# Counting GpSimd overlap in the assumed VectorE durations of a list-scheduled delta rule

## The chip, the cores and the metric

The kernel runs on one core of a Trainium2 chip, as one launch. The metric is the device time of that launch in microseconds (us), taken as the median of several executions. Besides the time there is one profiled execution, whose trace records every instruction of the core's engines: TensorE (PE, with its weight loads as PEld), VectorE (DVE), ScalarE (ACT), GpSimd (POOL) and SyncE (SP), which issues the DMA transfers.

## The reference

One inference step of a two-layer hybrid decoder, for a prompt of 1024 tokens and eight further sequences ("samples") of one token each. Layer one mixes by a gated delta rule with 8 heads of 128x128 state; layer two is a sliding-window attention over one shared K/V. The change lies in layer one alone:

```python
def gated_delta_rule(q, k, v, g, beta, s0):
    ...
    G = jnp.cumsum(gc, axis=-1)
    decay = jnp.exp(jnp.where(causal, G[..., :, None] - G[..., None, :], -jnp.inf))
    kb = kc * bc[..., None]
    m = jnp.where(strict, jnp.einsum('bnhid,bnhjd->bnhij', kb, kc) * decay, 0.0)
    rhs = jnp.concatenate([vc * bc[..., None], kb * jnp.exp(G)[..., None]], axis=-1)
    sol = lax.linalg.triangular_solve(eye + m, rhs, left_side=True, lower=True, unit_diagonal=True)
    ...
    def step(s, xs):
        u_i, w_i, qk_i, qd_i, kd_i, gt_i = xs
        v_new = u_i - jnp.einsum('bhcd,bhde->bhce', w_i, s)
        o_i = jnp.einsum('bhcd,bhde->bhce', qd_i, s) + jnp.einsum('bhij,bhje->bhie', qk_i, v_new)
        s = s * gt_i[..., None, None] + jnp.einsum('bhcd,bhce->bhde', kd_i, v_new)
        return s, o_i

def gdn_layer(x, conv_buf, s0, norm_g, w_in, conv_w, a_log, dt_bias, o_norm, w_out):
    proj = rmsnorm(x, norm_g) @ w_in
    qkv, gate, a, beta_logit = jnp.split(proj, [...], axis=-1)
    qkv, new_buf = causal_conv_silu(qkv, conv_buf, conv_w)      # 4 taps per channel
    ...                                                        # l2norm of q and k
    o, s_fin = gated_delta_rule(q, k, v, g, beta, s0)
    o = rmsnorm(o, o_norm) * jax.nn.silu(gate)
    return x + o @ w_out, new_buf, s_fin
```

The samples run through the same layer, each with a state of its own that is read from and written back to HBM.

## The kernel before, in words

**Stages.** Up to about 82 us the kernel loads and norms x and makes the first projections. From 82 to 752 us lies the delta-rule stage: the projections of all heads, the convolution, the delta rule, and the first part of the layer's output projection. From 752 to about 808 us the rest of that output projection runs for tiles of 128 tokens (loop over `P3O`, lines L1405 to L1455: `hx` is the residual tile, `ohl2` the split output of the last heads, `ohs` that of the samples). The attention layer takes the rest.

**Tiling of the delta-rule stage.** Each head's 1024 tokens are cut in chunks, and the chunks of a head are worked in two halves of four (512 columns on an engine); half n counts from 0 to 15 over the 8 heads. For a half, the convolution makes three taps each on VectorE (`co<-ue,cvT,co`, 528 columns) and two products on GpSimd (`ue<-ue,co`, `co<-co,ue`); the norms are small operations of four columns (`rs_x`, `rs_u`, `rkb`, `f`, `fu`); `ktok` is the normed k, transposed by TensorE into `ktp`; the triangular inverse is a series of `ivt` matmuls with `t`, `q` and `xlv` on VectorE between them; the chain over the chunks is the matmuls `chA` and `chB`; and the half's output `osb` is normed and transposed into `otp`. Everything else on TensorE is the *fill*: the projections `pj<-xg,whi`/`wlo` (weights split in a high and a low part by `whi` on ScalarE and `wlo` on VectorE), and at the end the output projection `pj<-woa,ohl` tile by tile.

**The order is a list made by the kernel itself.** The parts of the stage are generators (`chains`, `inverses`, `prep_all`, `norms`, `conv_all`, `feed`, `samples`, `proj_all`, ...) that yield one operation after the other. While the kernel is built, a class `Order` walks through them as a list scheduler. It holds for each engine the time `at[e]` until which it is busy, and for each tile when it was written and read last, by assumed durations (`took`). It always takes the operation that can start earliest by these times; ties go to the lower priority number (chains 1, convolution 5, `samples` 7, fill 9), and a TensorE operation that is not fill counts as ready 250 ns later. What it emits is the order of each engine's queue, so the assumed durations decide that order and nothing else. All these instructions carry the line of the one call that emits them, L543 (L558 after the change). The assumed duration of a convolution tap is 205 + 1.05*528 = 759 ns, whatever GpSimd does meanwhile.

**The samples' states.** `sample_batch` (lines L1147 to L1273), called by `samples` after heads 3 and 7, updates the states of four heads in eight units, each of 256 KB. Per unit: load `ssm` (SP), multiply by the decay (GpSimd, `ssm<-ssm,smp`), a matmul `up` (TensorE), add (VectorE, `ssm<-ssm,up`), store (SP, `out_7`). The tile `ssm` has two buffers, so a unit's load waits for the store of the unit two before. After the second batch's last add, VectorE's queue holds `ogm` (the samples' output), then the first `ohl2` and `hx` operations of the code behind the stage; SP's queue holds behind the last store the loads of the first four `hx` tiles. These orders behind the stage are fixed by the code.

Of the kernel before, what the change touches and what calls it, by code (L numbers as in the profile page):

```python
# [50 lines left out]
OPH = 400  # L51


D0, PEM, VF, DP = 12000.0, 250.0, 1.0, 2000


@with_exitstack
def hybrid_step(
# [9 lines left out]
    V, S, G, PE, DMA = nc.vector, nc.scalar, nc.gpsimd, nc.tensor, nc.sync  # L68
# [163 lines left out]
    with tc.tile_pool(name="p2a", reuse_waits="tile", bufs=1) as p2a, \  # L232
# [63 lines left out]
        for t in range(NT + 1):  # L296
# [9 lines left out]
            for hf in range(2):  # L306
                ps = gps("xps").rearrange("p (k t) -> p k t", k=4)
                for k in range(4):
# [4 lines left out]
                                in1=hi.bitcast(F32), op=ALU.subtract)  # L313
# [14 lines left out]
        with tc.high_priority(offset=DP):  # L328
# [29 lines left out]
            for kk in (15, 13, 11, 9, 7, 5, 3):  # L358
# [17 lines left out]
                            in1=rb.rearrange("p (c h) -> p c h", h=H), op=ALU.mult)  # L376
            psg = gps("psg")
            gfl = gf.rearrange("p h c -> p (h c)")
            for i, m in enumerate((mle, mgt, ones)):
# [8 lines left out]
                            in1=ident[:NS, :NS].unsqueeze(1).broadcast_to([NS, 2 * H, NS]), op=ALU.mult)  # L388
# [10 lines left out]
    class Op:  # L399
        __slots__ = ("e", "f", "a", "k", "use", "t")  # L400

        def __init__(self, e, f, a, k):
            self.e, self.f, self.a, self.k = e, f, a, k
            outs = [x for x in (k.get("out", a[0] if a else None), k.get("accum_out")) if x is not None]
            ins = [x for x in (*a[0 if "out" in k else 1:], *(y for n, y in k.items() if n not in ("out", "accum_out")))
                   if isinstance(x, bass.AP)]
            self.use = [(extent(x), True) for x in outs] + [(extent(x), False) for x in ins]
# [29 lines left out]
    def free_n(ap):  # L437
        n = 1
        for d_ in ap.shape[1:]:
            n *= d_  # L440
        return n

    def took(op):

        out = op.k["out"] if "out" in op.k else op.a[0]
        n = free_n(out)
        name = op.f.__name__
        if op.e == "P":
            src = op.a[2]
            n = free_n(src)  # L450
            if src.dtype == F16:
                return max(29, n / 2.4 + 2.5)
            t_ = n / 2.295 + 7 if n >= 256 else 109
            return t_ * (2 if name == "matmul" and src.dtype == F32 else 1)
        if op.e == "V":
            if name == "scalar_tensor_tensor" and n >= 64:
                return VF * (205 + 1.05 * n)
            if name == "tensor_tensor" or ap_psum(op):
                return VF * (150 + 1.04 * n)
            return VF * (150 + 0.65 * n)  # L460
        if op.e == "S":
            t_ = 165 + 0.83 * n
            if isinstance(op.k.get("scale"), bass.AP):
                t_ += 100
            return t_ + (235 if "accum_out" in op.k else 0)
        if op.e == "G":
            if name == "affine_select":
                return 130 + 1.25 * n
            if name == "tensor_tensor":
                return 100 + 2.35 * n  # L470
            return 100 + 0.8 * n if name == "memset" else 200 + 5 * n
        return 60

    def ap_psum(op):
        return any(x[0][0].space == PSUM for x in op.use)

    AFTER = {"P": 250.0, "V": 70.0, "S": 70.0, "G": 90.0}

    class Order:
        def __init__(self, slots, begin):  # L480
            self.slots, self.at = slots, dict(begin)
            self.toks = set()
            self.procs = []
            self.seen, self.rings, self.base = {}, {}, {}
            self.dma = 0.0

        def mark(self, *tok):
            self.toks.add(tok)
# [35 lines left out]

        def emit(self, op, t_):
            c_ = took(op)
            self.at[op.e] = t_ + c_
            if op.e == "D":
                n = 1
                for d_ in (op.k["out"]).shape:  # L530
                    n *= d_
                self.dma = max(self.dma, t_) + n * 4 / 180.0
                end = self.dma + 2000.0
            else:
                end = t_ + c_ + AFTER[op.e]
            for (tile_, *ext), write in op.use:
                w, rd = self.region(tile_, write).setdefault(tuple(ext), [("", 0.0), {}])
                if write:
                    self.seen[tile_.name][tuple(ext)][0] = (op.e, end)
                    rd.clear()  # L540
                else:
                    rd[op.e] = max(rd.get(op.e, 0.0), end)
            op.f(*op.a, **op.k)  # L543
# [859 lines left out]
    with tc.tile_pool(name="p3", reuse_waits="tile", bufs=2) as p3:  # L1403
# [4 lines left out]
        for t in P3O:  # L1408
# [13 lines left out]
            for ci in range(2):  # L1422
                c_ = ts(ci, 512)
# [20 lines left out]
            for hf in range(2):  # L1444
                ps = gps("hps").rearrange("p (k t) -> p k t", k=4)
                k0 = 4 * hf
                for k in range(4):
# [4 lines left out]
                                op=ALU.subtract)  # L1452
# [414 lines left out]
```

## Time and profile before

| | |
|---|---|
| time, median of 3 runs | 1298.4 us (1294.66 to 1300.23) |
| time of the profiled execution | 1299.52 us |
| its span | 1297.8 us |
| mean granted TensorE clock | 0.985 of full |
| delta-rule stage, 82 to 752 us | 670 us |
| rest of the output projection, 752 to 808 us | 56 us |

The span is what the trace covers; the execution's time is 1.7 us longer. "Granted clock" is the share of full TensorE speed that the chip let the engine run at. An engine's idle time is given with the instruction that ended it, its releaser; VectorE operations with a PSUM operand read what TensorE has just written, those without have all operands in SBUF.

### The profile page before, as it was taken

How to read it: one execution, taken by the hardware profiler on the slowest of the kernel's cores; microseconds unless marked ns; L12 is line 12 of the kernel's file. 1: busy time of each engine (PE TensorE's matmuls, PEld its weight loads, DVE VectorE, ACT ScalarE, POOL GpSimd, SP SyncE). 2: the span in 40 equal slices, each digit the busy share in tenths (PEclk: the TensorE clock that was granted, in tenths of full speed). 3: DMA queues.
4: the chain of work that ended last, by engine and by line, in shares of the span. 5: the costliest groups of instructions: out<-in, count | busy, mean ns of one | idle time of the engine just before them, and what ended most of it. 6: DMA issues, size and time to landing. Idle time of an engine off the chain costs nothing.

```text
span 1297.8 us, 24347 instructions
## 1 busy us (share of the span) xinstructions
PE 1223.9 (94%) x8887; PEld 1110.2 (86%) x8887; DVE 925.4 (71%) x2656; ACT 633.7 (49%) x1812; POOL 287.4 (22%) x404
## 2 busy tenths in 40 slices
PE   3999999999999999998999978999999999999998
PEld 3989898989999988888988756888889888888898
DVE  7468988878979897787976349587685677677221
ACT  5236555645455453545443127375574566666100
POOL 1036433424324353343301122111030020000000
PEclk9999999999999999998999979999999999999899
DMA  7021111110221322110256656111020021002322
GB/s 240 1 81 35 36 29 40 37 51 18 68 66 36 98 65 86 36 36 17 67 158 209 203 200 203 39 52 31 3 74 9 3 74 35 26 2 88 123 86 73
DMA packets 131988, 92.03 MB, mean 71 GB/s; under 512 B 33881, under 2 KB 123713, under 8 KB 131809
## 3 DMA queue, kind: packets, MB, share of 16 engines
q1 hardware_dynamic: 131868, 90.48, 23.6%
q8 instruction: 70, 1.15, 0.4%
q14 instruction: 50, 0.40, 0.1%
HBM read 69.28 MB, written 23.25 MB: 71 GB/s over the span
## 4 chain that ended last, share of the span: by engine, by line
PE 66%; DVE 20%; ACT 5%; DMA 4%; issue 3%; POOL 2%; SPq 1%; DVEq 0%; ACTq 0%; POOLq 0%
PE pj L543 24%; PE pj L100 15%; PE ivt L543 4%; DVE co L543 3%; PE chB L543 3%; PE sps L100 2%; PE chA L543 2%; PE op L100 2%; DMA out_dram<-hx 1%; PE ptp L1646 1%; DVE wqkv L82 1%; PE sp L543 1%; PE tq L1593 1%; DVE f L543 1%; PE psab L100 1%
## 5 line engine op out<-in xcount | busy, mean ns | idle before, releaser
L543 PE MATMUL pj<-xg,whi 128*128 128x384 f32 (+1 forms) x1392 | 289.3, 335 | 1.0 <-ACT whi L543 1.0
L543 PEld LDWEIGHTS pj<-xg,whi 128*128 128x128 f32 x1392 | 222.0, 190 | 2.7 <-ACT whi L543 1.2
L100 PE MATMUL pj<-wqkv,ng 128*128 128x384 f32 x768 | 154.2, 344 | 0.0
L543 PE MATMUL pj<-xg,wlo 128*128 128x384 f32 (+1 forms) x696 | 153.2, 337 | 0.0
L543 DVE SCALAR_TENSOR_TENSOR co<-ue,cvT,co 128x528 f32<-128x528 f32 x144 | 134.5, 940 | 16.1 <-ACT co L543 14.5
L100 PEld LDWEIGHTS pj<-wqkv,ng 128*128 128x128 f32 x768 | 132.3, 190 | 4.6 <-issue 4.2
L543 PEld LDWEIGHTS pj<-xg,wlo 128*128 128x128 f32 x696 | 112.9, 191 | 1.4 <-issue 0.7
L93 POOL TENSOR_TENSOR raw<-raw,gains 128x512 f32<-128x512 f32 x40 | 45.7, 1152 | 254.4 <-DMA raw<-in_w_in_b_dram 178.7
L100 PE MATMUL pj<-wob,oh 128*128 128x384 f32 (+1 forms) x576 | 97.9, 324 | 0.3 <-DVE hx L1828 0.3
L100 PEld LDWEIGHTS pj<-wob,oh 128*128 128x128 f32 x576 | 90.2, 190 | 1.1 <-DVE hx L1828 0.5
L543 PE MATMUL pj<-woa,ohl 128*128 128x512 f32 x288 | 76.1, 406 | 0.0
L543 PEld LDWEIGHTS pj<-woa,ohl 128*128 128x128 f32 x288 | 51.8, 188 | 11.5 <-issue 1.5
L1828 DVE TENSOR_TENSOR hx<-hx,pj 128x384 f32<-128x384 f32 (+3 forms) x27 | 13.7, 507 | 64.8 <-PE pj L100 35.8
L543 ACT COPY ue<-pj 128x384 f32<-128x384 f32 (+1 forms) x88 | 31.7, 377 | 52.8 <-PE pj L543 45.8
L543 POOL TENSOR_TENSOR ue<-ue,co 128x528 f32<-128x528 f32 x24 | 33.9, 1412 | 72.4 <-ACT ue L543 72.4
L543 DVE TENSOR_TENSOR wlo<-raw,whi 128x512 fp32r<-128x512 f32 x58 | 43.6, 757 | 7.6 <-ACT whi L543 7.4
L543 ACT ACTIVATE ue<-co 128x528 f32<-128x528 f32 x48 | 30.8, 644 | 30.2 <-DVE co L543 27.9
L543 ACT CAST whi<-raw 128x512 fp32r<-128x512 f32 x58 | 35.8, 619 | 16.9 <-PE pj L543 16.5
L100 PE MATMUL pj<-woa,ohl 128*128 128x512 f32 x96 | 28.7, 453 | 11.2 <-DVE ohl L1421 5.7
L543 POOL TENSOR_TENSOR co<-co,ue 128x528 f32<-128x528 f32 x24 | 39.0, 1623 | 1.3
L100 PE MATMUL sps<-kTh,qst 128*128 128x256 f32 (+1 forms) x144 | 37.5, 297 | 0.9 <-DVE m L1623 0.9
L100 PE MATMUL sps<-kTl,qst 128*128 128x256 f32 (+1 forms) x144 | 35.9, 297 | 0.5 <-DVE kTl L1600 0.5
(906 smaller groups left out, 2935.2 us busy)
## 6 DMA issues: line engine op xcount, KB each, us to landing
raw<-in_w_in_a_dram SPq DMA_DIRECT2D x64, 256.0 KB
ssm<-in_state_ssm_dram SPq DMA_DIRECT2D x32, 256.0 KB
hD<-hx SPq DMA_DIRECT2D x16, 512.0 KB
raw<-in_w_in_b_dram SPq DMA_DIRECT2D x32, 256.0 KB
xt<-in_x_prompt_dram SPq DMA_DIRECT2D x8, 512.0 KB
out_dram<-ssm SPq DMA_DIRECT2D x16, 256.0 KB
raw<-in_w_out_a_dram SPq DMA_DIRECT2D x16, 256.0 KB
hx<-in_x_prompt_dram SPq DMA_DIRECT2D x8, 512.0 KB
```

The source lines that it names most:

```text
L82: V.tensor_tensor(out=lo, in0=raw, in1=hi.bitcast(F32), op=ALU.subtract)
L93: G.tensor_tensor(out=raw, in0=raw, in1=gain[:, k:k + n].unsqueeze(2).broadcast_to([P, n, c]), op=ALU.mult)
L100: PE.matmul(out, lhsT, rhs, start=start, stop=stop, skip_group_check=True)
L543: op.f(*op.a, **op.k)
L1593: PE.transpose(tq[:, ts(h, P)], qhl[:, h].rearrange("p a d -> p (a d)"), identr)
L1646: PE.transpose(pp[:, ts(h, P)], pr[h // 2][:, h % 2, ts(kt, P)], ident)
L1828: V.tensor_tensor(out=hx[:n, :cn], in0=hx[:n, :cn], in1=ps[:n, :cn], op=ALU.add)
```

## The change

Two things are added. `shares_port` picks GpSimd's two-operand and select operations, and those VectorE operations that have a second tensor input (`in1`) and no operand in PSUM. `emit` keeps the assumed intervals of the last four such GpSimd operations, and lengthens the assumed duration of such a VectorE operation by HOLD = 0.6 of its overlap with each of them, where the operation counts as at least 500 ns long for the overlap. GpSimd's own assumed durations stay.

```diff
-D0, PEM, VF, DP = 12000.0, 250.0, 1.0, 2000
+D0, PEM, VF, DP, HOLD = 12000.0, 250.0, 1.0, 2000, 0.6
...
+    def shares_port(op):
+
+        if op.e == "G":
+            return op.f.__name__ in ("tensor_tensor", "affine_select")
+        return op.e == "V" and "in1" in op.k and not ap_psum(op)
+
...
+            self.held = []
...
         def emit(self, op, t_):
             c_ = took(op)
+            if shares_port(op):
+                if op.e == "G":
+                    self.held = self.held[-3:] + [(t_, t_ + c_)]
+                else:
+                    for b_, e_ in self.held:
+                        over = min(t_ + max(c_, 500.0), e_) - max(t_, b_)
+                        if over > 0.0:
+                            c_ += HOLD * over
             self.at[op.e] = t_ + c_
```

No instruction is added, removed or altered; only their order within the delta-rule stage moves, on every engine. Three places:

TensorE, half n = 6 (first half of the fourth head), the rows that stand behind the chain's last `chB`, as far as the transpose `otp` of the half's output (the number behind a name is that of the tile's allocation). Before:

```order
L543 MATMUL aps_5041<-co_4754,kT_5007 128x128 x2
L543 MATMUL pj_4951<-xg2_99,whi_4469 128x264
L543 MATMUL sp_5052<-kq_4734,ssm_5025 128x2 x4
L543 MATMUL pj_4951<-xg2_99,whi_4469 128x264 x3
L543 MATMUL kps_5079<-ident_78,co_4489 128x128 x4
L543 MATMUL pj_4951<-xg2_99,whi_4469 128x264 x2
L543 MATMUL pj_5101<-xg0_97,whi_4676 128x384 x4
L543 MATMUL dps_5118<-gm_5074,mgtr_116 128x512
L543 MATMUL pj_5101<-xg0_97,whi_4676 128x384 x4
L543 MATMUL pj_5101<-xg0_97,wlo_4677 128x384
L543 MATMUL dps_5118<-gm_5077,mgtr_116 128x512
L543 MATMUL otp_5125<-ident_78,osb_4875 128x128 x4
```

The same place of the changed kernel, where two fill matmuls of 264 columns, behind the same `chB`, stand ahead of these rows:

```order
L558 MATMUL qps_4964<-ident_78,co_4809 128x128 x4
L558 MATMUL pj_4930<-xg2_99,whi_4511 128x264 x8
L558 MATMUL pj_4992<-xg0_97,whi_4774 128x384 x8
L558 MATMUL pj_4992<-xg0_97,wlo_4775 128x384 x8
L558 MATMUL ktp_5036<-ident_78,ktok_4913 128x128 x4
L558 MATMUL pj_4992<-xg0_97,whi_4774 128x384 x8
L558 MATMUL pj_5062<-xg1_98,whi_4774 128x384 x2
L558 MATMUL nps_5055<-kT_5041 128x128 x4
L558 MATMUL dps_5077<-gm_4980,mgtr_116 128x512
L558 MATMUL dps_5077<-gm_4983,mgtr_116 128x512
L558 MATMUL pj_5062<-xg1_98,whi_4774 128x384 x2
L558 MATMUL otp_5086<-ident_78,osb_4782 128x128 x4
```

Between `chB` and `otp` stand 15 fill matmuls before (6 of 264 columns, 9 of 384) and 38 now (10 and 28).

TensorE, the end of the stage: the last fill (`pj<-woa1,ohl`), the `up` matmuls of the second sample batch, and the first matmul of the code behind the stage. Before:

```order
L543 MATMUL pj_9541<-woa0_8253,ohl_9487 128x512 x14
L543 MATMUL up_9565<-db_9455,kl_9054 128x512
L543 MATMUL pj_9541<-woa0_8253,ohl_9487 128x512 x4
L543 MATMUL pj_9572<-woa1_8404,ohl_9487 128x512 x18
L543 MATMUL up_9598<-db_9455,kl_9054 128x512
L543 MATMUL up_9603<-db_9455,kl_9054 128x512
L100 MATMUL pj_9639<-woa2_8663,ohl2_9636 128x512 x6
```

And in the changed kernel:

```order
L558 MATMUL pj_9512<-woa0_8199,ohl_9470 128x512 x7
L558 MATMUL up_9528<-db_9419,kl_9385 128x512
L558 MATMUL pj_9512<-woa0_8199,ohl_9470 128x512 x11
L558 MATMUL pj_9544<-woa1_8336,ohl_9470 128x512 x18
L558 MATMUL up_9568<-db_9419,kl_9385 128x512
L558 MATMUL up_9573<-db_9419,kl_9385 128x512
L558 MATMUL up_9584<-db_9577,kl_9385 128x512
L558 MATMUL up_9591<-db_9577,kl_9385 128x512
L558 MATMUL up_9598<-db_9577,kl_9385 128x512
L558 MATMUL up_9603<-db_9577,kl_9385 128x512
L100 MATMUL pj_9639<-woa2_8477,ohl2_9636 128x512 x6
```

Of the batch's eight `up` matmuls two stood behind the last fill before, and six do now; six and two stand within the fill.

SP, the same place: state loads (`ssm<-in_state_ssm`), state stores (`out_7`), the store of the last `hx` tile of the stage, weights of the next layer (`raw`), and the first `hx` load of the code behind. Before:

```order
L543 DMA hD_88<-hx_9486 128x1024
L543 DMA ssm_9575<-in_state_ssm_dram 128x4x128
L543 DMA out_7_dram<-ssm_9525 128x4x128
L91 DMA raw_10195<-in_w_in_b_dram 128x4x128
L91 DMA raw_10200<-in_w_in_b_dram 128x4x128
L91 DMA raw_10205<-in_w_in_b_dram 128x4x128
L543 DMA out_7_dram<-ssm_9575 128x4x128
L91 DMA raw_10210<-in_w_in_b_dram 128x4x128
L1413 DMA hx_9634<-hD_88 128x1024
```

And in the changed kernel, behind the three `raw` loads, which stand where they did:

```order
L558 DMA out_7_dram<-ssm_9537 128x4x128
L558 DMA ssm_9579<-in_state_ssm_dram 128x4x128
L91 DMA raw_10210<-in_w_in_b_dram 128x4x128
L558 DMA ssm_9581<-in_state_ssm_dram 128x4x128
L558 DMA out_7_dram<-ssm_9579 128x4x128
L558 DMA ssm_9588<-in_state_ssm_dram 128x4x128
L558 DMA out_7_dram<-ssm_9581 128x4x128
L558 DMA ssm_9595<-in_state_ssm_dram 128x4x128
L558 DMA out_7_dram<-ssm_9588 128x4x128
L558 DMA out_7_dram<-ssm_9595 128x4x128
L1428 DMA hx_9634<-hD_88 128x1024
```

Four more loads and four more stores now stand ahead of the `hx` loads.

## Rows read from the trace of the kernel before

**Rows 1.** The page's first part: busy time, share of the span and instructions, by engine.

```profile
PE 1223.9 (94%) x8887; PEld 1110.2 (86%) x8887; DVE 925.4 (71%) x2656; ACT 633.7 (49%) x1812; POOL 287.4 (22%) x404
```

**Rows 2.** Table by stage: window, length, busy time, granted clock, DMA share, GB/s.

```profile
82.00:752.00 670.00, 645.96 (x5246) 593.51 (x5247) 538.57 (x1156) 328.30 (x973) 229.48 (x326) 0.99 0.24 70
752.00:808.00 56.00, 43.33 (x191) 30.08 (x192) 39.12 (x124) 29.54 (x51) 13.88 (x18) 0.88 0.69 214
```

**Rows 3.** TensorE's waits from 82 to 752 us: total, times, longest.

```profile
PE ivt L543 <- DVE t L543: 3.7, 4, 1.7
PE otp L543 <- DVE m L543: 3.3, 3, 2.1
PE otp L543 <- DVE osb L543: 2.2, 2, 1.4
PE ktp L543 <- DVE ktok L543: 2.2, 1, 2.2
PE ivt L543 <- DVE q L543: 2.1, 3, 0.9
PE ivt L543 <- DVE xlv L543: 1.7, 2, 1.4
...
PE otp L543 <- DVE vt L543: 1.4, 1, 1.4
```

**Rows 4.** Table by stretch, two stretches of reduced clock in the delta-rule stage.

```profile
553.00:556.40 3.40, 3.40 (x17) 3.40 (x16) 2.63 (x4) 0.87 (x2) 3.00 (x3) 0.50 0.03 5
...
590.50:597.30 6.80, 5.91 (x38) 5.60 (x38) 6.70 (x11) 1.00 (x3) 0.84 (x4) 0.50 0.29 77
```

**Rows 5.** VectorE's operations of L543: shortest/median/longest in ns, first and last start.

```profile
L543 DVE SCALAR_TENSOR_TENSOR co<-ue,cvT,co x144: 750/768/1847, 57.0 to 621.8; 128x528 f32<-128x528 f32 x144
...
L543 DVE TENSOR_TENSOR xlv<-ivt,lm x32: 676/691/693, 134.9 to 658.4; 128x512 f16<-128x512 f32 x32
...
L543 DVE TENSOR_SCALAR rs_x<-ssq x16: 155/162/1305, 101.2 to 631.5; 128x4 f32<-128x4 f32 x16
```

**Rows 6.** Timeline at 479 to 487 us, GpSimd, VectorE and TensorE: start, length, operation, [idle before].

```profile
479.47 1.33 POOL L543 TENSOR_TENSOR ue<-ue,co 128x528 f32<-128x528 f32 x1 [4.87 <-ACT ue L543]
479.52 1.30 DVE L543 TENSOR_SCALAR rs_x<-ssq 128x4 f32<-128x4 f32 x1
486.03 0.65 PE L543 MATMUL ktp<-ident,ktok 128*128 128x128 f32 x4 [2.17 <-DVE ktok L543]
```

**Rows 7.** Timeline of TensorE at half n = 6, last chain matmul and output transpose.

```profile
386.58 0.39 PE L543 MATMUL chB<-w,dt 128*128 128x128 f32 x2
392.45 0.63 PE L543 MATMUL otp<-ident,osb 128*128 128x128 f32 x4 [0.92 <-ACT jk L543]
```

**Rows 8.** The page's costliest group: busy time, mean ns of one, idle before.

```profile
L543 PE MATMUL pj<-xg,whi 128*128 128x384 f32 (+1 forms) x1392 | 289.3, 335 | 1.0 <-ACT whi L543 1.0
```

**Rows 9.** Timeline at the stage's end, of TensorE, SP, GpSimd and VectorE, in order of time.

```profile
745.68 0.50 PE L543 MATMUL up<-db,kl 24*128 24x512 f32 x1
746.11 5.40 PE L543 MATMUL pj<-woa,ohl 128*128 128x512 f32 x22
752.71 0.38 SPq L543 DMA_DIRECT2D ssm<-in_state_ssm_dram  x1
756.49 1.04 POOL L543 TENSOR_TENSOR ssm<-ssm,smp 128x512 f32<-128x512 f32 x1 [8.05 <-DMA ssm<-in_state_ssm_dram]
757.56 0.69 DVE L543 TENSOR_TENSOR ssm<-ssm,up 128x512 f32<-128x512 f32 x1 [4.73 <-POOL ssm L543]
758.80 3.78 PE L100 MATMUL pj<-woa,ohl 128*128 128x512 f32 x8 [5.73 <-DVE ohl L1421]
759.30 2.38 SPq L1413 DMA_DIRECT2D hx<-hD  x4
765.12 1.28 DVE L1434 TENSOR_TENSOR hx<-hx,pj 128x512 f32<-128x512 f32 x2
765.95 9.26 PE L100 MATMUL pj<-woa,ohl 128*128 128x512 f32 x28 [3.37 <-DVE hx L1434]
```

## The prediction, made before the changed kernel was run

> **What bounds the kernel now.** I read the page's busy times first. TensorE works 94% of the span, VectorE 71%, GpSimd 22% [rows 1], so what a new order can change on the whole is TensorE's idle time. The table by stage then tells where there is any: from 82 to 752 us, where the change acts, TensorE is busy 645.96 of 670.00 us, 24.0 us idle; from 752 to 808 us, behind it, it is busy 43.33 of 56 us [rows 2]. The table of waits names what the 24 us are: TensorE waits for the steps of the inverse on VectorE (`ivt` for `t`, `q`, `xlv`: 3.7 + 2.1 + 1.7 = 7.5 us), for what stands on VectorE ahead of an output transpose (`otp`: 3.3 + 2.2 + 1.4 = 6.9 us), once for `ktok` (2.2 us), and for little besides [rows 3]. Two stretches of the stage run at half of the granted clock (0.50, the 1.2 of 1.2 and 2.4 GHz), right after such stalls, 3.40 and 6.80 us long [rows 4]. At full clock their work would take half, so (3.4 + 6.8)/2 = 5.1 us more are lost. The stage thus has 24.0 + 5.1 = 29 us to give at most.
>
> Does the cause that the change assumes exist? The list of VectorE's operations says so: a tap takes 768 ns in the median, near the 759 that the scheduler assumes, but up to 1847; the norm's `rs_x` takes 162 ns and up to 1305; while `xlv`, which reads PSUM, stays between 676 and 693 [rows 5]. The timeline shows how: `rs_x` starts at 479.52 and ends at 480.82, just behind GpSimd's `ue`, which ran from 479.47 to 480.80. A small operation was held for the whole of GpSimd's, and the `ktok` that hangs on it came 2.17 us late for TensorE [rows 6].
>
> **The change, part by part.** No work is added, so each term is one of place.
>
> *Stalls in the stage.* Where VectorE's operations are now assumed longer, what hangs on them is ordered later, and fill takes their place. Half n = 6 is the example. Before, TensorE comes to `otp` 392.45 − 386.58 = 5.87 us after the last chain matmul and has waited 0.92 of it [rows 7]; so 4.95 us of work stood between. The changed order puts 23 more fill matmuls there. One costs 289.3/1392 = 0.208 us [rows 8], 23 cost 4.8, which covers 0.92 several times. By the same count for all 16 halves, the work ahead of `otp` grows where halves 3 to 8 wait, and I count 5 us of the 6.9 us of `otp` waits as gone. The inverse's steps stand in the new order about as far from each other as before, so their 7.5 us and `ktok`'s 2.2 shrink by a third at most: 2 us counted, since where one overlap goes another comes. Of the 5.1 us of half clock, which hang on single stalls, I count 2. Sum −9 us. Bounds: 0, if new stalls take the place of the old; −29, if all is found.
>
> *The tail.* This is the part for which the change was not made. Before, two `up` matmuls stand behind the last fill, now six. A unit's cost where nothing covers it is in the timeline: its load is issued at 752.71, GpSimd begins at 756.49, VectorE's add ends at 757.56 + 0.69 = 758.25, 5.54 us from issue to sum [rows 9]. Before, the last unit ends there, the first split of the output (`ohl`), next in VectorE's queue, follows, and TensorE resumes at 758.80 after 5.73 us of waiting; then the four `hx` loads, which stand on SP behind the last store, go out at 759.30, the add to the first starts at 765.12, and TensorE resumes at 765.95 after 3.37 more [rows 9]. In the changed order the unit that ends at 758.25 is only the fourth of eight, and loads have two buffers, each freed by the store of the unit two before:
> unit 5: its load stands right behind that unit's store, so it goes out at about 758.7 and its sum is ready at 758.7 + 5.5 = 764.2;
> unit 6: its load waits for the landing of unit 4's store, issued at about 758.3. No row shows a store's landing alone. Below it is 0, above it is a load's way to its first user, 756.49 − 752.71 = 3.8 us [rows 9]; I take the middle, 2. Sum at 760.3 + 5.5 = 765.8;
> unit 7: waits for unit 5's store, 764.3 + 2, sum at 771.8;
> unit 8: waits for unit 6's store, 765.9 + 2, sum at 773.4.
> TensorE's first resumption moves from 758.80 to 773.4 + 0.55 = 774.0. The `hx` loads go out at about 774; before, the first was used 765.12 − 759.30 = 5.8 us after issue, with weights' transfers ahead of it and GpSimd late for the `ohs` next in VectorE's queue; alone it may take a load's 3.8 us. I take 4.4, and 0.83 from the add to TensorE as before: 779.2 against 765.95, **+13.2 us**. Bounds: no time for the store and 3.8 for `hx`, 775.6, +9.7; 3.8 for the store and 5.8 for `hx`, 784, +18. TensorE's work there stood behind long waits before too, at a granted clock of 0.88 in the mean [rows 2], so the clock is counted at no difference.
>
> *Less work ahead of the tail.* Four `up` matmuls leave the fill; one cost 746.11 − 745.68 = 0.43 us there [rows 9], in the tail they hide in waits: −1.7 us.
>
> *The second batch's reading of the states* (`sp`) now comes tens of matmuls before the end instead of hundreds, with loads that have little ahead of them. What covers them is the fill of one tile; if that is gone one load's 3.8 us shows. I take +1, bounds 0 and 4.
>
> Sum: 13.2 − 1.7 + 1 − 9 = +3.5 us on the profiled execution's 1299.5, so 1303.0. That execution is 1.1 us above the median of 1298.4, so against the median: **1302 us**.
>
> **The rivals.**
>
> *A. Stalls hardly shrink, and the tail costs its price (slower).* The rows show a block of a whole GpSimd operation: 1.30 us for work of 0.16 [rows 5, 6]. The change assumes 0.6 of an overlap, takes a small operation as 500 ns, and leaves out `rs_x`, which has one input only. What was to be late stays late, by less. Then the stalls give 3 and not 9: 13.2 − 1.7 + 1 − 3 = +9.5, 1308 us. The Trainium skill, "SBUF — State Buffer", section "Who interferes with whom", states this mechanism: VectorE's second pair of ports is GpSimd's, the lock on it is exclusive, whoever issues first has it for the whole instruction and the other fully blocks, and single-input operations such as tensor_scalar can take the pair too. The trace agrees in the 1.30 us of `rs_x`; by that rule an overlap costs all of the rest of the other engine's instruction, and its time would be rival A's 1308. For it: the rows above, and that GpSimd's own waiting is in neither list. Against it: more distance helps whatever its reason, and half n = 6 has five times what it lacked.
>
> *B. The stage gives back most of its stalls (faster).* All `otp` and `ktok` waits, half of the inverse's and all of the half clock would be 6.9 + 2.2 + 3.8 + 5.1 = 18, and with the smaller waits some 22: 13.2 − 1.7 + 1 − 22 = −9.5, 1289 us. It decides from the point where the stage gives more than 12.5 + 6.5 = 19 us. For it: all stalls hang on VectorE's being late, which is what the change teaches the list. Against it: it needs two thirds of all that there is, and a new list makes stalls of its own.
>
> *C. The tail is hidden (faster or same).* If the loads go out earlier than I work out, or the later waits behind 766 us shrink since the weights are there by then, the tail costs 5 in place of 13: 5 − 1.7 + 1 − 9 = −5, 1294 us. For it: a DMA share of 0.69 from 752 to 808 us [rows 2], so transfers are a part of those waits. Against it: two buffers, and the stores ahead of them, tie every load to the sum of two units before, whatever the bandwidth.
>
> **How the numbers follow.** About 0.5%, 6.5 us, is what a measurement of this kernel can tell from no change: 1291.9 to 1304.9. Forecast (stalls give 6 to 15, tail 10 to 16): 0.46, most of it within that bound and a part above. A: 0.27. B: 0.12. C: 0.15, half of it under 1291.9. Faster then 0.12 + 0.06 = 0.18; slower 0.27 and 0.09 of the forecast, 0.36; same 0.46. The range reaches from C's lower part to A with the tail's upper bound: 1290 to 1312; the forecast alone has 1296 to 1307.
>
> **What the changed profile would show.** The tail right: TensorE's wait for `ohl` (then L1436) of 18 to 24 us in place of 5.73, SP's issues of `ssm` loads there about 2 and 6 us apart in turn, TensorE's busy share from 752 us on lower by a fifth. The stalls right: TensorE's idle time from 82 us to the last fill at 15 us in place of 24, the `otp` waits under 2 us, the ends of the fill about 8 us earlier. Wrong: idle time of 20 us or more there (A), of under 8 (B), or TensorE's second resumption less than 8 us after the first `up` plus 14.5, as before (C). What would undo the whole working is a change in TensorE's busy time itself, which I have as equal, since its instructions are.

## The result, and the profile after

The changed kernel takes 1315.97 us in the median of 4 executions (1312.5 to 1320.2), the kernel before 1297.91, also of 4: a ratio of 1.0139, 95% interval 1.0118 to 1.0160. It is slower by 18 us, outside the range that was given, on the side of rival A but beyond it. The profiled execution took 1317.07 us, its span is 1315.3. In e1 to e4 below an execution of 1.5 to 4.6 times the usual time (one each of e1, of e3 and of the kernel before) is left out of the median.

The table by stage, with a window that ends with the fill (columns as in [rows 2]):

```profile
82.00:749.50 667.50, 645.32 (x5241) 593.74 (x5241) 531.72 (x1152) 329.75 (x973) 228.09 (x321) 0.99 0.23 67
```

TensorE is idle for 667.5 − 645.3 = 22.2 us in the stage, against 24.0 [rows 2]. So the idle time of the stage hardly changed, and the loss came behind it. The clock did not change there either: as in [rows 4], one stretch of 3.4 and one of 6.8 us stand at half clock, elsewhere than before (columns as there):

```profile
519.00:522.40 3.40, 2.80 (x25) 2.64 (x26) 1.26 (x2) 1.43 (x3) 0.66 (x1) 0.50 0.92 266
532.70:539.50 6.80, 6.30 (x22) 6.04 (x23) 5.27 (x9) 2.08 (x7) 1.89 (x5) 0.50 0.00 0
```

The waits of TensorE in the stage, now (columns as in [rows 3]):

```profile
PE dps L558 <- POOL gm L558: 2.2, 2, 1.4
PE ivt L558 <- ACT xlv L558: 1.6, 1, 1.6
PE chB L558 <- DVE rr L558: 1.6, 1, 1.6
PE chA L558 <- DVE st L558: 1.5, 4, 0.8
PE otp L558 <- DVE osb L558: 1.4, 1, 1.4
...
PE chB L558 <- ACT qs L558: 1.3, 4, 0.7
PE chB L558 <- DVE rs_u L558: 1.1, 1, 1.1
...
PE ivt L558 <- DVE t L558: 1.0, 3, 0.6
...
PE otp L558 <- DVE m L558: 0.8, 1, 0.8
```

The list of [rows 3] is another list now. `ktp` for `ktok` has gone from it, `otp` waits 1.4 + 0.8 us here where it waited 6.9, and in their place the chain matmuls `chA` and `chB` wait for `rr`, `st`, `qs` and `rs_u`. Before, they hardly waited:

```profile
PE dps L543 <- POOL gm L543: 1.5, 2, 1.3
...
PE chB L543 <- ACT qs L543: 0.7, 3, 0.3
...
PE chA L543 <- DVE st L543: 0.6, 1, 0.6
```

The VectorE operations themselves are as stretched as in [rows 5]:

```profile
L558 DVE SCALAR_TENSOR_TENSOR co<-ue,cvT,co x144: 751/766/1922, 57.0 to 630.2; 128x528 f32<-128x528 f32 x144
...
L558 DVE TENSOR_SCALAR rs_x<-ssq x16: 156/168/1253, 101.6 to 632.2; 128x4 f32<-128x4 f32 x16
```

The end of the stage, TensorE's timeline (columns as in [rows 9]):

```profile
742.04 7.03 PE L558 MATMUL pj<-woa,ohl 128*128 128x512 f32 x29
749.00 0.50 PE L558 MATMUL up<-db,kl 24*128 24x512 f32 x2
756.19 0.79 PE L558 MATMUL up<-db,kl 24*128 24x512 f32 x2 [6.69 <-POOL db L558]
762.00 0.79 PE L558 MATMUL up<-db,kl 24*128 24x512 f32 x1 [5.01 <-DVE ssm L558]
763.99 0.79 PE L558 MATMUL up<-db,kl 24*128 24x512 f32 x1 [1.20 <-DVE ssm L558]
764.71 2.08 PE L100 MATMUL pj<-woa,ohl 128*128 128x512 f32 x4
773.45 3.78 PE L100 MATMUL pj<-woa,ohl 128*128 128x512 f32 x8 [6.66 <-DVE ohl L1436]
778.12 8.47 PE L100 MATMUL pj<-woa,ohl 128*128 128x512 f32 x28 [0.89 <-DVE hx L1449]
786.43 1.04 PE L1463 MATMUL hps<-ident,hn 128*128 128x128 f32 x8
```

Of the six `up` matmuls behind the fill the first two run at once; then TensorE waits four times, 6.69 + 5.01 + 1.20 us for the others and 6.66 for `ohl`, and 0.89 for `hx`, where 5.73 and 3.37 stood in [rows 9]. From the fill's end to the second resumption it is 778.12 − 749.07 = 29.0 us; before it was 765.95 − 751.5 = 14.5. SP's queue shows why:

```profile
755.89 0.38 SPq L558 DMA_DIRECT2D out_dram<-ssm  x1
756.33 0.50 SPq L558 DMA_DIRECT2D ssm<-in_state_ssm_dram  x1
...
759.03 0.37 SPq L558 DMA_DIRECT2D ssm<-in_state_ssm_dram  x1
761.97 0.38 SPq L558 DMA_DIRECT2D out_dram<-ssm  x1
764.28 0.37 SPq L558 DMA_DIRECT2D ssm<-in_state_ssm_dram  x1
764.75 0.45 SPq L558 DMA_DIRECT2D out_dram<-ssm  x1
768.05 0.37 SPq L558 DMA_DIRECT2D ssm<-in_state_ssm_dram  x1
769.53 3.77 SPq L558 DMA_DIRECT2D out_dram<-ssm  x2
773.40 1.91 SPq L1428 DMA_DIRECT2D hx<-hD  x4
```

A load follows the store that frees its buffer by 2.3 to 3.3 us (761.97 to 764.28, 764.75 to 768.05), and the `hx` loads go out last, at 773.40 against 759.30 [rows 9]. VectorE's first add to `hx` then waits for TensorE and not for the load:

```profile
777.29 1.28 DVE L1449 TENSOR_TENSOR hx<-hx,pj 128x512 f32<-128x512 f32 x2 [2.72 <-PE pj L100]
```

The profiled executions' difference, 17.5 us of span, splits like this, from TensorE's timeline of both (the attention layer is counted from its first projection of the prompt's tokens, `pj<-wqkv,ng`):

| stretch | before | after | difference |
|---|---|---|---|
| 82 us to the fill's end | 669.5 | 667.1 | −2.4 |
| fill's end to the first `hps` transpose | 23.5 | 37.4 | +13.9 |
| from there to the first projection of the attention layer | 35.7 | 35.6 | −0.1 |
| attention layer to the end | 487.1 | 493.4 | +6.3 |

### The profile page after: what moved, and what is told of

The parts are those of the page before. It is cut to its first block, busy times and chain, and to the rows that moved or that the text cites. A ratio compares the mean times of both kernels' runs of the same rounds, so it can differ in the third digit from the quotient of the medians.

```text
span 1315.3 us, 24356 instructions
## 1 busy us (share of the span) xinstructions
PE 1228.9 (93%) x8887; PEld 1114.4 (85%) x8887; DVE 922.0 (70%) x2656; ACT 635.3 (48%) x1812; POOL 289.9 (22%) x404
## 4 chain that ended last, share of the span: by engine, by line
PE 67%; DVE 16%; ACT 6%; DMA 5%; issue 3%; POOL 2%; SPq 1%; DVEq 0%; ACTq 0%; POOLq 0%
PE pj L558 26%; PE pj L100 15%; PE ivt L558 4%; PE chB L558 3%; PE sps L100 2%; DVE co L558 2%; PE chA L558 2%; PE op L100 2%; DMA out_dram<-hx 1%; PE ptp L1661 1%; DVE wqkv L82 1%; PE sp L558 1%; PE nps L558 1%; DMA hx<-hD 1%; DMA ssm<-in_state_ssm_dram 1%
## 5 line engine op out<-in xcount | busy, mean ns | idle before, releaser
L558 PE MATMUL pj<-xg,wlo 128*128 128x384 f32 (+1 forms) x696 | 149.7, 335 | 0.0
L558 DVE SCALAR_TENSOR_TENSOR co<-ue,cvT,co 128x528 f32<-128x528 f32 x144 | 134.0, 938 | 14.4 <-ACT co L558 12.8
L558 PE MATMUL pj<-woa,ohl 128*128 128x512 f32 x288 | 79.4, 410 | 0.4 <-ACT ohl L558 0.4
L1843 DVE TENSOR_TENSOR hx<-hx,pj 128x384 f32<-128x384 f32 (+3 forms) x27 | 13.7, 508 | 66.2 <-PE pj L100 41.0
L558 ACT CAST whi<-raw 128x512 fp32r<-128x512 f32 x58 | 35.8, 619 | 18.5 <-PE pj L558 18.0
L100 PE MATMUL pj<-woa,ohl 128*128 128x512 f32 x96 | 28.8, 454 | 9.5 <-DVE ohl L1436 6.7
L558 ACT COPY w<-chB 128x128 f32<-128x128 f32 x64 | 17.0, 265 | 42.8 <-PE chB L558 42.1
```

Of the source, the lines that this page charges most:

```text
L100: PE.matmul(out, lhsT, rhs, start=start, stop=stop, skip_group_check=True)
L1843: V.tensor_tensor(out=hx[:n, :cn], in0=hx[:n, :cn], in1=ps[:n, :cn], op=ALU.add)
```

## The experiments

The columns "stage idle" (TensorE's idle time from 82 us to the fill's end), "tail" (fill's end to first `hps`) and "attention" are read from the timeline of each run's profiled execution as in the table above. Times are medians; the ratio is to the kernel before, run beside it. That kernel took 1295 to 1298 us in these rounds, so compare ratios rather than times. In the row of e3 and e15 the time is e3's, the rest that of e15's one execution, which took 1310.0 us.

| run | us | ratio, 95% interval | fill's end | stage idle | `up` behind fill | tail | attention |
|---|---|---|---|---|---|---|---|
| before | 1297.9 | | 751.5 | 24.0 | 2 | 23.5 | 487.1 |
| after | 1316.0 | 1.0139 [1.0118, 1.0160] | 749.1 | 22.2 | 6 | 37.4 | 493.4 |
| e1 after again | 1312.2 | 1.0115 [1.0066, 1.0164] | 749.0 | 22.3 | 6 | 36.9 | 493.0 |
| e2 tail alone | 1311.0 | 1.0103 [1.0066, 1.0140] | 748.6 | 23.9 | 6 | 35.8 | 486.6 |
| e3, e15 after, prefetch | 1305.8 | 1.0068 [1.0047, 1.0090] | 758.3 | 26.4 | 4 | 23.1 | 490.5 |
| e4 before, prefetch | 1300.5 | 1.0020 [1.0004, 1.0036] | 751.9 | 22.4 | 4 | 23.0 | 487.8 |
| e5 VectorE 2% longer | 1318.1 | 1.0182 [1.0147, 1.0217] | 762.2 | 30.3 | 5 | 32.4 | 485.8 |
| e6 full lock | 1358.2 | 1.0492 [1.0453, 1.0530] | 800.6 | 46.5 | 6 | 37.3 | 486.8 |
| e7 HOLD 0.3 | 1302.4 | 1.0061 [1.0043, 1.0080] | 750.6 | 23.0 | 4 | 27.0 | 485.7 |
| e8 samples early | 1311.2 | 1.0115 [1.0072, 1.0158] | 771.9 | 37.4 | 0 | 9.2 | 490.5 |
| e9 after, batch 2 at 1.3 | 1309.2 | 1.0122 [1.0066, 1.0177] | 763.3 | 27.6 | 2 | 22.6 | 488.4 |
| e10 HOLD 0.3, batch 2 at 0.5 | 1293.4 | 0.9987 [0.9970, 1.0003] | 760.2 | 26.9 | 0 | 9.2 | 484.1 |
| e11 before, batch 2 at 1 | 1289.6 | 0.9952 [0.9928, 0.9976] | 756.2 | 26.1 | 0 | 9.2 | 484.9 |
| e12 before, batch 2 at 2.1 | 1292.1 | 0.9976 [0.9960, 0.9992] | 759.6 | 27.9 | 0 | 9.2 | 483.8 |
| e13 after, 4 fills late | 1312.2 | 1.0111 [1.0080, 1.0142] | 747.9 | 21.4 | 6 | 37.0 | 489.4 |
| e14 after, 8 fills late | 1318.0 | 1.0147 [1.0127, 1.0167] | 749.7 | 21.2 | 6 | 40.2 | 491.3 |

**e1, the changed kernel again.**

> The changed kernel once more, unaltered. Its first profile was 17.5 us over before: the fill of the delta-rule stage ended 2.4 us earlier, TensorE's second resumption behind the samples' tail came 12.2 us later, and the attention layer, whose order is the same, took 6.2 us more, in stretches of half clock at 842, 1226 and 1242 us that before had not or had elsewhere. Theory A (the attention layer's extra time is chance of one execution): the profile here has an attention layer (from the first pj<-wqkv to the end) within 2 us of before's, and the median lies near 1310. Theory B (it belongs to the new timing): the same stretches of half clock at the same places again, 5 to 7 us more than before from 808 us on, and a median of 1314 to 1318.

Stage and tail came out the same to 0.5 us, and the attention layer took 493.0 us again. One stretch of half clock, that behind 842 us, was gone, and that at 984 was longer. So the layer's length is not the chance of one execution, and theory B is borne out in that; but the stretches of half clock are chance in part, and the median, 1312.2 us, lies 2 us under B's and as far above A's.

**e2, the tail alone.** Tokens hold the second batch back in the list of before:

```diff
+                if h0:
+                    u_ = 4 * hb + hh
+                    yield from need(("filled",) if u_ > 1 else ("of", NT - 2 + u_))
                 yield from get("gen")
                 up = gps("up")
...
         for t in range(NT):
+            mark("of", t)
...
         yield from out_all()
+        mark("filled")
```

> The list of before, with the second sample batch alone held back by tokens until it stands at the stage's end as in the changed kernel: two of its up matmuls in the last two tiles of the fill, six behind it, with SP's order there as in the changed kernel. Theory A (the tail is most of the loss, whatever the rest of the list): second resumption of TensorE 29 us after the first up behind the fill, as in the changed kernel (before: 14.5), so 14.5 less 1.7 for the four up matmuls that leave the fill gives 12 to 13 us more, 1310 us; up to 1316 if the attention layer's extra time comes with the tail's delay too. Rival (the loss lies in the stage's own new stalls, which the tail only hides): within 4 us of before, 1302 or less.

TensorE's timeline of this kernel:

```profile
755.64 0.80 PE L543 MATMUL up<-db,kl 24*128 24x512 f32 x2 [6.65 <-POOL db L543]
761.44 0.79 PE L543 MATMUL up<-db,kl 24*128 24x512 f32 x1 [5.01 <-DVE ssm L543]
...
772.92 3.72 PE L100 MATMUL pj<-woa,ohl 128*128 128x512 f32 x8 [6.69 <-DVE ohl L1426]
777.73 6.78 PE L100 MATMUL pj<-woa,ohl 128*128 128x512 f32 x28 [1.08 <-DVE hx L1439]
```

With no overlap counted, and TensorE's order that of before as far as the second batch, the waits for `db`, `ssm` and `ohl` are those of the changed kernel to 0.1 us and the second resumption to 0.4 us. By the medians the tail alone costs 13 us (9 to 18 by the interval), by the profiled executions 9 (a span of 1306.5 against 1297.8). By the profiles the rest of the changed kernel's 17.5 us is the attention layer, which takes 486.6 us here; the medians of this round, 1.0103 here and 1.0115 in e1, do not tell the two kernels apart.

**e3, e4, e15, prefetch.** The second batch's loads go out up to five units ahead, into eight buffers, so that no load waits for a store:

```diff
+        tags = ["ssm"] * 8 if not h0 else ["ssm", "ssm", "kd", "kd", "at", "at", "vt", "vt"]
...
+        ahead = 5 if h0 else 1
+        nxt = 0
+        for u, (hb, hh) in enumerate(un2):
+            while nxt < 8 and nxt <= u + ahead:
+                yield again(nxt)
+                nxt += 1
```

> The changed kernel, with the loads of the second sample batch's update issued up to five units ahead, into buffers of the delta rule that are free by then, so that no load waits for a store; five up matmuls still stand behind the fill. Theory A (the tail costs by its loads and stores): TensorE's waits for db, ssm and ohl there shrink from 19.6 us in all to under 7, its second resumption comes 10 to 12 us after the first up in place of 29, and the time falls to 1296 to 1303. Rival (VectorE, GpSimd and up matmuls themselves take the time): 1310 or more.

> The kernel before, with the same prefetch of the second sample batch; by its list four up matmuls stand behind the fill in place of two. Theory A: the two waits of 5.7 and 3.4 us shrink by 3 to 5 us together, since no load is left there, 1293 to 1297 us. Rival (the tail is bound by the hx loads behind it): no change, 1298.

> The changed kernel with the prefetch of the second batch's states, which gave 1305.9 us, for its profile. Theory A (the tail is what the prefetch takes out): the fill ends within 3 us of the changed kernel's 749 us, and from there to the first hps transpose it is 23 to 28 us in place of 37. Rival (the gain comes from another place, the stage or the attention layer): 35 us or more there.

(e3's list has four `up` matmuls behind the fill, not five.) In the changed kernel the waits for `db`, `ssm` and `ohl` fall from 19.6 to 0.95 us and the tail from 37 to 23.1, as theory A has it; the ratio falls from 1.0139 (e1: 1.0115) to 1.0068, 6 to 9 us. The rest of A missed: the second resumption comes 14.2 us behind the first `up` and not 10 to 12, the time is 1305.8 and not 1303 or less, and the fill ends 9 us later, 4 of it idle, so the stage took back a part. In the kernel before the prefetch gains nothing, as the rival said. TensorE's timeline of that run (e4):

```profile
755.72 2.13 PE L100 MATMUL pj<-woa,ohl 128*128 128x512 f32 x8 [0.22 <-DVE ohl L1429]
766.44 8.59 PE L100 MATMUL pj<-woa,ohl 128*128 128x512 f32 x28 [8.58 <-DVE hx L1442]
```

The wait of 5.73 us for `ohl` is gone, and that for `hx` has grown from 3.37 to 8.58 [rows 9]: what stands last on SP, the `hx` loads, sets the end.

**e5, a list that is other by a hair.**

```diff
-D0, PEM, VF, DP = 12000.0, 250.0, 1.0, 2000
+D0, PEM, VF, DP = 12000.0, 250.0, 1.02, 2000
```

> The kernel before, with no count of overlaps, but all assumed VectorE durations 2% longer: a list that is other by a hair, as a measure of what any new list does. By its rows five up matmuls stand behind the fill (before two, the changed kernel six). Theory A (a new list moves TensorE's stalls rather than removing them, and the tail sets the time): TensorE idle 20 to 27 us from 82 us to the end of the fill, the fill's end within 3 us of 749 to 752, a tail some 10 us longer than before's, in all 1305 to 1313 us. Rival (the counted overlaps did change the stage, by as much as they lost): idle time and fill's end the same as before to 1 us.

At least as slow as the changed kernel, with nothing known of overlaps: 30.3 us idle and five `up` matmuls behind the fill. The rival fell, and theory A's numbers (up to 27 us idle, a fill end by 755 us, 1313 us) were all too low. That the list of before has only two `up` matmuls behind the fill was luck as far as these lists go: no count of overlaps put them where they are.

**e6, the overlap as the timeline shows it.**

```diff
+            if op.e == "G" and shares_port(op) or op.e == "V" and not ap_psum(op):
+                s_ = max(t_, self.lock)
+                c_ += s_ - t_
+                self.lock = t_ + c_
```

> The count of overlaps taken the way the timeline shows them: a VectorE operation without a PSUM operand and a GpSimd two-operand or select operation exclude each other, the later one starts when the earlier has ended, single-input operations and GpSimd's own waiting included. Five up matmuls stand behind the fill. Theory A (stalls move from place to place in any list): TensorE idle 18 to 27 us in the stage, 1305 to 1314 us in all. Rival (0.6 of an overlap was too little, the stalls would go with the true length): idle 12 us or less in the stage, the fill's end at 740 us or before, 1296 to 1303 us.

(Six stand behind the fill.) The rival fell, and far, and theory A's numbers with it: the idle time doubled, and stretches of 89 us in sum ran at half clock, where before and after it was 10.2. Its row by stage, and TensorE's longest waits there:

```profile
82.00:800.60 718.60, 672.10 (x5241) 615.85 (x5241) 528.71 (x1151) 328.67 (x974) 227.59 (x321) 0.94 0.21 62
```

```profile
PE dps L554 <- POOL gm L554: 8.2, 1, 8.2
PE otp L554 <- DVE osb L554: 5.2, 2, 3.3
PE ivt L554 <- DVE xlv L554: 4.1, 5, 1.4
```

**e7, HOLD = 0.3** in place of 0.6.

> The changed kernel with HOLD = 0.3 in place of 0.6; four up matmuls behind the fill in place of six. Theory A: two units fewer in the tail, one round of store and load (some 7 us) less than the changed kernel, the stage's idle time 20 to 27 us without order: 1305 to 1311 us. Rival (the stage gains with the counted overlap and 0.6 was too much or too little): an idle time of 15 us or less, or 30 or more.

The stage's idle time is 23.0 us, between those of no count and of 0.6. The time is 3 us under what was expected, with the kernel before 3 us lower too in this round (1295.1) and an attention layer of 485.7 us, not more than before; the tail is 10 us shorter than at 0.6.

**e8, both sample batches early.**

```diff
-                          ..., (7, samples()), (FILL, proj_all())):
+                          ..., (1, samples()), (FILL, proj_all())):
```

> The kernel before, with no count of overlaps, with the samples' generator at priority 1 in place of 7: no up matmul is left behind the fill. Theory A (each unit behind the fill costs, the two of before as well): TensorE's wait of 5.7 us for ohl is gone, its second resumption, set by the hx loads, comes 9 to 11 us after the end of the fill in place of 14.5; 1292 to 1296 us if the stage's idle time stays at 24. Rival (the early batch pushes the delta rule's own work back): idle time of 28 us or more in the stage, and 1298 us or more.

Both effects came. TensorE goes on without a wait where the fill ends, so the tail is 9.2 us, 14 less than before (theory A had left a wait for `hx`), and the stage's idle time is 37.4 us, 13 more, as the rival has it; the second outweighs the first.

**e9 to e12, the second batch alone early.**

```diff
-            if h % 4 == 3:
-                yield from sample_batch(h - 3)
+            if h == 3:
+                yield from sample_batch(0)
+            elif h == 7:
+                spawn(1, sample_batch(4))
```

with priority 1.3 and HOLD = 0.6 (e9), 0.5 and HOLD = 0.3 (e10), 1 and 2.1 in the kernel before (e11, e12).

> The changed kernel with HOLD = 0.6, the second sample batch alone at priority 1.3 in place of 7: the list is the changed kernel's up to the batch (the first 3655 rows of TensorE's 5020), and behind the fill stand two up matmuls, as before, in place of six. Theory A (the tail is the loss): from the fill's end to the first hps transpose 23 to 26 us in place of 37, the stage's idle time 22 to 26 us, 1299 to 1305 us. Rival (the stage's new stalls are the loss, or the batch brings as many when it comes earlier): 1310 us or more, with an idle time of 30 us or more.

> HOLD = 0.3, the second sample batch alone at priority 0.5: no up matmul behind the fill, the last one eleven rows ahead of it. Theory A: the time from the fill's end to the first hps transpose falls from 27 us to 9 to 12, as where both batches came early; with an idle time in the stage of 23 to 27 us the whole is 1284 to 1291 us, less than both kernels. Rival (VectorE's and GpSimd's work for the batch then pushes back the last chains, which stand on the path): idle time over 33 us, 1298 us or more.

> The kernel before, no overlaps counted, the second sample batch alone at priority 1: the list of before up to row 3644 of TensorE, no up matmul behind the fill, the last one five rows ahead of its end. Theory A: from the fill's end to the first hps transpose 9 to 12 us in place of 23.5, idle time 24 to 28 us, 1284 to 1290 us. Rival (as for HOLD = 0.3): idle time over 33 us, 1298 us or more.

> The kernel before, the second sample batch at priority 2.1: behind the chains, the inverses and the preparation, ahead of the convolution. No up matmul behind the fill, the last one three rows ahead of its end, so its store is just under way when the fill ends. Theory A: the first hps transpose 12 to 16 us behind the fill, idle time 24 to 27 us, 1287 to 1292 us. Rival: as there, 1298 us or more.

In e9 the tail was undone, 22.6 us, yet the fill ended 14 us later. So theory A's time missed, and the rival's bounds (1310 us, 30 us idle) were nearly reached, by its second reason: the earlier batch cost 5 us of idle time and a stretch of reduced clock from 655 to 676 us (0.59). It doesn't speak for new stalls of the changed list, whose fill ends at 749. In e10 to e12 the tail is 9.2 us each, and the fill ends 5 to 10 us later; the rivals, with idle times over 33 us, fell. e11 came as theory A has it and beats both kernels, by 0.5% the one before. e10 and e12 lie at or above the upper end of A's times: e10 cannot be told from the kernel before, and e12 gains 0.2%. e11's timeline on TensorE and SP:

```profile
740.81 15.42 PE L543 MATMUL pj<-woa,ohl 128*128 128x512 f32 x65
756.07 9.50 PE L100 MATMUL pj<-woa,ohl 128*128 128x512 f32 x40
```

```profile
741.69 0.38 SPq L543 DMA_DIRECT2D out_dram<-ssm  x1
...
743.10 0.86 SPq L1415 DMA_DIRECT2D hx<-hD  x2
```

With the last store out at 741.69, the first `hx` loads go out at 743.10, within the fill, and TensorE passes from the fill to the next matmuls without a wait.

**e13, e14, the changed kernel with a delay behind the samples' last sum.**

```diff
+        if h0:
+            late = gd.tile(B4, F32, tag="at", name="late", bufs=NB)
+            for _ in range(4):
+                yield vq.memset(late, 0.0)
```

> The changed kernel with four fills of a free tile (512 columns each) on VectorE behind the last sum of the samples' states, so that what follows starts later by one to two us, all orders as in the changed kernel. Its two executions gave an attention layer of 493.4 and 493.0 us from its first projection, before's 487.1, and that of the tail alone 486.6. Theory A (the extra 6 us hang on where the attention layer's VectorE operations fall against GpSimd's weights and the transfers, and with it on when it begins): another start gives another time, 484 to 491 us, and the whole comes out at 1308 to 1316 in spite of the delay. Theory B (they belong to the changed list whatever the start): 493 us again, 1315 to 1319 in all.

> The same with eight fills, a start later by two to three us. Theory A: an attention layer of 484 to 491 us, not the same as with four by more than 1 us. Theory B: 493 us, 1316 to 1320 in all.

The attention layer takes 489.4 and 491.3 us, shorter than without a delay and not alike, as theory A has it; but 491.3 is just over its bound, and e14's total is theory B's. Nor was the delay what it was meant to be: in e13's profile the tail is no longer (37.0 us) and the layer begins at 820.1 us, 1.9 earlier than in the changed kernel, in e14's 3.1 later. The start was moved in both, but these two alone don't decide between A and B. What the profiles add is in the next section.

## Why the prediction was wrong

**The tail was right, in mechanism and nearly in size.** The second resumption was put 13.2 us later than before, on a fill end that stays; counted from the fill's end it came 29.0 − 14.5 = 14.5 us later. Two errors cancel in part. The store's landing, taken as 2 us, was 2.3 to 3.3 from issue to issue, so the last sum came 23.8 us behind the fill's end (at 772.90) and not 21.9; and the `hx` loads were in time, so that the add to the first waited for TensorE and not for them, and it took 5.2 us from there to the resumption and not 5.8. The sign "TensorE's wait for `ohl` of 18 to 24 us" did not come as worded: that wait is 6.66 us, and three waits of `up` matmuls stand ahead of it, 19.6 in sum. The `ssm` loads went out 2.7, 5.3 and 3.8 us apart, not 2 and 6 in turn. TensorE's busy share from 752 to 808 us fell from 0.77 to 0.65, near the fifth that was given. e2 shows that this tail costs 9 to 13 us by itself, with no overlap counted.

**The step that failed is *Stalls in the stage*, −9 us.** The fill ended 2.4 us earlier and not about 8. With the four `up` matmuls at their 1.7, as the prediction has them, 0.7 is left for stalls and the `sp` term, where −9 + 1 was expected. The count of 5 us for `otp` was right: it waits 2.8 us in all where it waited 8.3 with its small entries. `ktp` and the inverse lost 4.6 more, where 2 was counted. But `chA` and `chB`, with 1.7 us of waits before, now have 7.0, and `dps` 3.2 for 1.5, so that the idle time fell by 1.8 in all. And of the half clock, counted at −2, nothing came: its two stretches are as long as before. The sentence "a new list makes stalls of its own" stood among the rivals, and in the term only as its bound of 0. With the term at that bound the sum is 13.2 − 1.7 + 1 = 12.5 us and the time 1311, still inside the range; what takes the time out of it is the attention layer, below. By the mark set there, 20 us or more of idle time, this is rival A; its reason is not borne out, though: the `otp` and `ktp` stalls did go, e6 counts the whole block and has twice the idle time, and e5 changes the list for no reason and has 30.3 us.

The Trainium skill, "SBUF — State Buffer", section "Who interferes with whom", on which rival A drew, has the later of two such operations blocked until the other engine's has ended. The traces agree on that: in the changed kernel a `qt` of 8x256 takes 1.29 us at 836.26, right under GpSimd's pair at 835.16, and 0.41 us elsewhere. As a cost in this list (e6) it did harm.

**A term was missing: the attention layer, +6 us.** Its order of instructions is the same, and the text counted it at nothing, with TensorE's busy time as equal. That rose from 1223.9 to 1228.9 us: 3.0 of it in this layer, 2.5 in the tail. The layer's idle time rose by 3.2. TensorE's waits there that differ, the changed kernel first:

```profile
PE ktps L1748 <- DMA kc__14947<-in_cache_k_win_dram: 2.9, 1, 2.9
PE gps__10406 L100 <- DVE oT L1539: 2.1, 1, 2.1
```

```profile
PE gps__10406 L100 <- DVE oT L1524: 1.5, 1, 1.5
...
PE ktps L1733 <- DMA kc__14947<-in_cache_k_win_dram: 0.9, 1, 0.9
```

The longer waits, 2.6 us more together in the changed kernel, stand in each of the five profiles whose list is the changed kernel's as far as the second batch (`ktps` 2.6 to 2.9, `oT` 2.0 to 2.1 in e1, e9, e13, e14), and in no other (`ktps` at most 1.6, `oT` 1.5 or 1.6). For `oT` the timeline shows the way: GpSimd's second pair of weights falls on VectorE's `qt`, in the kernel before on two later operations.

```profile
835.16 2.11 POOL L93 TENSOR_TENSOR raw<-raw,gains 128x512 f32<-128x512 f32 x2 [1.07 <-DVE rs_u L132]
```

```profile
836.26 1.29 DVE L1572 TENSOR_TENSOR qt<-s_qkv,r 8x256 f32<-8x256 f32 x1
```

The other half of the 6 us is the clock. In the kernel before 14.4 us of the layer stand at half clock, in the changed one 21.5. Half of that time is lost, so 3.6 us more. Two of these stretches begin by such a wait, within the windows 842 to 848 us (0.72 in the mean) and 1225 to 1229 (0.59):

```profile
842.00:848.00 6.00, 6.00 (x29) 5.99 (x29) 0.47 (x2) 1.07 (x3) 0.00 (x0) 0.72 0.00 0
...
1225.00:1229.20 4.20, 3.23 (x15) 3.14 (x16) 0.00 (x0) 1.18 (x2) 0.00 (x0) 0.59 0.73 263
```

That the waits cause the lower clock is not shown: e1 has the `oT` wait (2.1 us) without the stretch behind it, e9 and e13 have both waits and 13.7 and 15.0 us at half clock, e8 has neither and 24.1. So the waits go with the list, as theory B of e13 and e14 has it, and the clock varies from run to run, as theory A has it.

For `ktps` it is the load that takes longer. From the issue of the `kc` load to its first use it is 7.1 to 7.6 us in the five profiles and 5.3 to 5.9 in all the others of the table. In the changed kernel and in e2 it is issued at

```profile
1218.36 0.41 SPq L1741 DMA_DIRECT2D kc__14947<-in_cache_k_win_dram  x1
```

```profile
1213.15 0.40 SPq L1731 DMA_DIRECT2D kc__14947<-in_cache_k_win_dram  x1
```

and first used at 1225.96 and 1218.75. Why transfers land otherwise with this list stays open. It is not the order on the queue, which is the same in e2 from the `hx` loads on, nor when the layer begins: e13 begins it at 820.1 us and e2 at 819.9, and only e13 has the waits.

**Rivals B and C** did not come: the idle time fell by 1.8 us, and neither bandwidth nor later waits gave the tail back (the stretch behind it took 35.7 us before and 35.6 after).

## What to carry to other kernels

A list made from assumed durations is moved as a whole by any of its numbers; read first which work it pushes to the end of the stage, where nothing covers it, and what the queue of transfers holds behind that work. A truer duration is no gain by itself: here the count of overlaps, in three strengths, left TensorE's idle time at 22 to 46 us, and moving one small generator's priority (e11) gained 0.5%, by the tail and not by the stage's idle time. Before a stage's waits are counted as gain, ask which instruction waits in their place; without an answer, count the sum of waits as unchanged.

## What was not expected of the hardware

The same sequence of instructions in the attention layer took from 483.8 to 493.4 us in the profiles of the table, with waits that depend on when GpSimd works on the next weights and when the cache `kc` lands, and with half-clock stretches, some of which begin at waits of 2 to 3 us (the waits that end at 841.65 and 1225.96 in the changed kernel, the stretches at 843.3 and 1225.6). The same load of the cache, in the same place of the queue, took 7.1 to 7.6 us to its first use with one list and 5.3 to 5.9 with all others. The loop of load, multiply, add and store over two buffers gave two units in 8 to 9 us (loads at 756.33 and 759.03, then at 764.28 and 768.05), and 2.3 to 3.3 us of that are a store's way to a free buffer.
